# A two-layer hybrid transformer block: more block sums on VectorE, and chunk 3 of the last three feed-forward nets by seven block products

## The chip, the core and the metric

One core of a Trainium2 chip runs the whole program: two layers, batch 1, 256 tokens, all data in fp32. The core has five engines that run side by side, each with its own in-order stream of instructions: TensorE (PE, matrix products into PSUM; its weight loads appear as PEld), VectorE (DVE), ScalarE (ACT), GpSimd (POOL) and SyncE (SP, which here only issues transfers). Transfers run on 16 DMA engines. The metric is the device time of one execution in microseconds; the time of a kernel is the median of its runs.

## The reference

Each layer has a gated feed-forward net, a mixer (short convolution, a gated linear recurrence, multi-scale pooling), cross attention to 256 memory rows, and a second gated feed-forward net, each followed by a layer norm. The change touches the four feed-forward nets alone (two in each layer):

```python
D_MODEL = 1024; SEQ = 256; DEPTH = 2; D_FF = 2816

def swiglu(x, w_gate, w_up, w_down):
    return (jax.nn.silu(x @ w_gate) * (x @ w_up)) @ w_down

h = layer_norm(ALPHA * h + 0.5 * swiglu(h, ffn1_gate[l], ffn1_up[l], ffn1_down[l]), ln_g[l, 0], ln_b[l, 0])
...
h = layer_norm(ALPHA * h + 0.5 * swiglu(h, ffn2_gate[l], ffn2_up[l], ffn2_down[l]), ln_g[l, 3], ln_b[l, 3])
```

## The kernel before

**Products in three parts.** A weight block arrives in fp32 from memory. ScalarE rounds it to the matmul's fp32r type (the high part, tile `whi`, line 75) and VectorE subtracts that from the original (the low part, tile `wlo`, line 76). This pair is called a split here. A product is then the sum of three matmuls (high by high, high by low, low by high; `mm_rows`, line 132 through `product`). A split handles 128 x 1024 numbers, and there are eight `whi` and eight `wlo` buffers, so that ScalarE and VectorE can be at most eight splits ahead of TensorE.

**A feed-forward net.** The hidden width of 2816 is cut into five chunks of 512 (0 to 4) and one of 256 (chunk 5). For each chunk the kernel makes gate and up products with the 256 tokens (two tiles of 128), gates them, turns them (through a small transfer, `dealt`, and a transpose on VectorE into `square`), splits the result into `ah` and `al`, and later multiplies it by two slabs of the down matrix (`both`, four splits for the two slabs), which accumulate in four PSUM banks named `dn`. All other products go to the four PSUM banks named `acc`.

**Plain chunks.** `hidden` makes a chunk by 16 steps of gate and 16 of up: 96 matmuls of 512 columns and 8 splits.

**Chunks by seven block products.** `by_seven` uses a Strassen-like form. The two tiles of tokens, the two halves of the model width, gate and up give a 2 by 2 block product; seven products of blocks of tokens with blocks of weights take the place of eight. The sums of token blocks (`bx`, kept in `kTh` and `kTl`) are made once a net. The sums of weight blocks are made for each chunk, and every sum is split anew: 14 splits and 84 matmuls for 512 columns. With g0, g1 for the two halves of gate (`w00`, `w10`) and u0, u1 for those of up (`w01`, `w11`), the products take, in this order, g0; g0+u0; g1; g0+u0+u1; u0+u1; u1; g0+u0+u1+g1 (for chunk 5 the fifth and the sixth change places). VectorE makes g0+u0 and then adds u1, in place (`plus` in `parts_of`, line 736). u0+u1 is made by a transfer that GpSimd issues, which reads u1 from memory a second time and adds it onto u0 in SBUF (`more`, line 772). For the last sum another such transfer adds g1 in chunks of 512, and VectorE in chunk 5. Two slabs of the down product (`between`) lie between the products of each seven.

**Which chunks.** `sevens` says which: 2 and 4 in the first net, 2, 4 and 5 in the other three. `later` says after which plain chunk how many slabs of the down product follow.

**Where blocks are kept.** The four weight blocks of a seven have rotating homes: the pairs `spare0`/`spare1` and `lng`/`lnb`, and buffers of the pool `raw` (six); the first half of `w10` lies in `spare2`. A block loaded into a home must wait until the block before it there was last read.

**Order.** A scheduler places the instructions of each engine; inside an engine they run in that order. Transfers by SP run in the order of its queue too, and a queue entry whose home is not yet free holds up those behind it.

Of the kernel before, what the change touches and what calls it, by code (L numbers as in the profile page):

```python
# [60 lines left out]
def model(ctx: ExitStack, tc: tile.TileContext, t: dict, out: bass.AP):  # L61
# [6 lines left out]
    def acc(shape=(P, 2, SEQ), tag="acc"):  # L68
        return ps.tile(list(shape), F32, tag=tag, name=tag)
# [4 lines left out]
    def split(hi, lo, src):  # L74
        rounded = nc.scalar.copy(hi, src)  # L75
        lows.append(nc.vector.tensor_tensor(lo, src, hi.bitcast(F32), op=ALU.subtract))  # L76
        return rounded
# [78 lines left out]
    def mm_rows(o, xh, xl, wh, wl, start, stop, more=False):  # L156
        product(o, xh, wh, start, False, more)
        product(o, xh, wl, False, False, more)
        product(o, xl, wh, False, stop, more)
# [350 lines left out]
    def ffn(l, name, n, pend=None, last=False, early=None, started=None, following=None):  # L510
        gate, up, down = (t[f"{name}_{x}"][l] for x in ("gate", "up", "down"))
        with tc.tile_pool(name="ffn", bufs=2, reuse_waits="tile") as fp:
            acts = []
# [185 lines left out]
            def by_seven(c0, ncol, bx, between):  # L699
                deep = 1024 // ncol  # L700

                def rows_by_columns(r):
                    return r.rearrange("p (k c) -> p k c", c=ncol)

                def pieces(*tags):
                    return [
                        rows_by_columns(
                            (fp if "spare" in g else wp).tile([P, DM], F32, tag=g, name="raw", bufs=6 if g == "raw" else 1)
                        )
                        for g in tags  # L710
                    ]

                def part_of(m, j, i):
                    k = 4 * j + deep * i
                    return m[k * P : (k + deep) * P, c0 : c0 + ncol].rearrange("(k p) c -> p k c", p=P)

                def block(m, j, to):
                    for i, x in enumerate(to):
                        loads.append(nc.sync.dma_start(x, part_of(m, j, i)))
                    return to  # L720
# [8 lines left out]
                w01 = block(up, 0, pieces(*homes[1]))  # L729
                w10 = block(gate, 1, pieces(*homes[3]))  # L730

                def parts_of(r, plus=None):
                    hi, lo = [], []
                    for i in range(len(r)):
                        if plus is not None:
                            nc.vector.tensor_tensor(r[i], r[i], plus[i], op=ALU.add)
                        h = wp.tile([P, 1024], F32R, tag="whi", name="whi", bufs=8)
                        w = wp.tile([P, 1024], F32R, tag="wlo", name="wlo", bufs=8)
                        h, w = (rows_by_columns(x) for x in (h, w))
                        split(h, w, r[i])  # L740
                        hi.append(h)
                        lo.append(w)
                    return Weights(hi, lo, deep, [])

                def part_of_x(i, j):
                    d = slice(4 * j, 4 * j + 4)
                    return xTh[:, d, tok(i)], xTl[:, d, tok(i)]

                def run(o, x, w, more=False):
                    for k in range(4):  # L750
                        wh, wl = w.at(k, slice(0, ncol))
                        mm_rows(o, x[0][:, k, :], x[1][:, k, :], wh, wl, k == 0 and not more, k == 3, more)

                def put(o, a, op, b):
                    nc.vector.tensor_tensor(ordered(o), ordered(a), in_order(b), op=op)  # L755
# [8 lines left out]
                def bank():  # L764
                    return acc((P, CHUNK))[:, 0:ncol]

                def taken(o, bank):
                    return nc.scalar.copy(ordered(o), in_order(bank))

                def more(to, m, j):  # L770
                    for i, x in enumerate(to):
                        nc.gpsimd.dma_start(x, part_of(m, j, i), accum_op=ALU.add)  # L772

                o, total, one = (bank() for _ in range(3))
# [1 line left out]
                nc.scalar.copy(total, o)  # L776
                run(one, bx[0], parts_of(w00, w01))
                taken(e, one)
                more(w01, up, 1)
                run(o, part_of_x(0, 1), parts_of(w10), True)  # L780
                between[0]()
                activate(s, 0, o)
                w11 = block(up, 1, pieces(*homes[2]))
# [4 lines left out]
                copied = nc.scalar.mul(less, total, -1.0)  # L788
                between[1]()
                if ncol == CHUNK:  # L790
                    run(total, bx[2], parts_of(w01), True)
                    put(f, e, ALU.subtract, total)
                    run(less, bx[3], parts_of(w11), True)
                    run(total, part_of_x(1, 1), parts_of(w00), True)
                else:
                    run(less, bx[3], parts_of(w11), True)
                    run(total, bx[2], parts_of(w01), True)
                    put(f, e, ALU.subtract, total)
                    with tc.issue_after(copied.ins):
                        w = parts_of(w00, w10)  # L800
                    between[2]()
                    run(total, part_of_x(1, 1), w, True)
# [42 lines left out]
            def slab(c, u, fine=False):  # L845
                w = load(down, c * 4 + 2 * u, 2, 0, DM, fine, dealt=c < len(chunks) - 1)
                ah, al = acts[c]
                return w, ah[:, 2 * u : 2 * u + 2, :], al[:, 2 * u : 2 * u + 2, :]


            sevens = (2, 4) if early is not None else (2, 4, 5)
            passed, dealts, turn_memory = [], [], None
            bx = []

# [14 lines left out]
            def both(c, u, a=None, steps=range(2)):  # L869
                a = a or slab(c, u)  # L870
                for i in range(NT):
                    for k in steps:
                        for m in range(2):
                            apart = last and i == m == k == u == 1 and c == 3
                            rows_of(a, i, k, m, c == u == k == 0, apart)

            todo = [(c, u) for c in range(4) for u in range(2)]
            later = (0, 0, 0, 2, 0, 2) if early is None else (0, 1, 0, 1, 0, 2)
            for c, (c0, ncol) in enumerate(chunks):
                if not c:  # L880
                    acts.append(first()())
                    ys = [[acc((P, 512), "dn") for _ in range(2)] for _ in range(NT)]
                elif c in sevens:
                    half = []

                    def deal_last():
                        acts[4] = acts[4]()

                    left = by_seven(
                        c0, ncol, bx,  # L890
                        [lambda: both(*todo.pop(0))] * 2 if ncol == CHUNK else
                        [lambda: (half.append(slab(3, 0)), both(3, 0, half[0], (0,))), deal_last, lambda: both(3, 0, half[0], (1,))],
                    )
                else:
                    acts.append(hidden(c0)() if ncol == CHUNK else last_hidden(c0, turn_memory))
                if c == 1 and early is None:
                    bx.extend(blocks_of_x())
                if c == 5:
                    gb = ln_params(l, n)
                if c == 1 and early is not None:  # L900

                    with tc.issue_after(loads[-1].ins):
                        rest = early(fp)
                if c == 3 and early is not None:
                    with tc.issue_after(lows[-1].ins):
                        rest[0]()
                    nc.gpsimd.tensor_copy(early_memory[:, 0:2048:256], acts[2][0][:, 0, 0:8].bitcast(F32))
                    turn_memory = load_memory(fp, loads[-1])
                if c in sevens:
                    if ncol < CHUNK:  # L910
                        held = []
                        with tc.issue_after(lows[-1].ins):
                            acts[4] = acts[4](held)
                    acts.append(left() if c + 1 in sevens else left()() if c == 5 else left()()())
                    if ncol < CHUNK:
                        with tc.issue_after(passed[-1][0].ins), tc.issue_after(passed[-1][1].ins):
                            held[0]()
                        both(3, 1)
                else:
                    for _ in range(later[c]):  # L920
                        both(*todo.pop(0))
# [589 lines left out]
```

## Time and profile before

| what | value |
|---|---|
| median of 3 runs | 1061.81 us (1061.22 to 1062.94) |
| the profiled execution, its own time | 1062.18 us |
| its span, from the first to the last instruction | 1060.5 us |
| mean granted TensorE clock | 0.998 |
| second, third and fourth net, from the transposes of their input to those of the next stage's (chain of waits) | about 361 to 528, 528 to 695, 884 to 1053 us |

In the tables by stretch a cell is busy us and, in brackets, instructions; PEclk is the granted clock as a share of full speed, DMA the busy share of the 16 DMA engines, and the last number GB/s. In a timeline a row is start, duration, engine, line, operation, tile written and tile read; what stands in square brackets is idle time before it and what ended it. A group's row ends with its idle time and the releasers. Matmuls overlap, so that a TensorE instruction's own duration (0.38 us) is longer than its step (see the chain). A row in the list of waits is: waiting engine, tile and line, what released it, us in total, times, longest.

### The profile page before, as it was taken

The numbers are of one execution on the slowest core, as the hardware profiler recorded it, in microseconds if no ns is written. First come the engines' busy times: TensorE is split into PE (matmuls) and PEld (weight loads), VectorE is DVE, ScalarE is ACT, GpSimd is POOL, SyncE is SP. The second block draws the span as 40 slices with busy tenths as digits, with TensorE's granted clock in tenths as the row PEclk, the third lists the DMA queues.
The fourth block names the chain that finished last, engine by engine and source line by source line (L and its number), as shares of the span: only waits on it lengthen the run. The fifth ranks groups of instructions, "written<-read, shape, count | busy, mean of one in ns | idle before, by whom it ended". The sixth has DMA issues, their size and how long they took to land.

```text
span 1060.5 us, 16438 instructions
## 1 busy us (share of the span) xinstructions
PE 1050.7 (99%) x5998; PEld 933.9 (88%) x5998; DVE 920.6 (87%) x1228; ACT 667.3 (63%) x917; POOL 99.6 (9%) x137
## 2 busy tenths in 40 slices
PE   9999999999999999999999999999999999999997
PEld 7888888989899888888888888998898998888896
DVE  6998898989898789897898887999898888898787
ACT  6675765677557556655675656666775665675661
POOL 8002001000100001010001001010001000000001
PEclk9999999999999999999999999999999999999999
DMA  9999984855675589988789988876637775799972
GB/s 362 297 284 298 271 276 147 260 174 160 216 261 202 167 280 227 348 208 224 239 297 260 336 220 216 266 233 227 200 114 237 250 240 170 242 288 307 237 198 70
DMA packets 142690, 252.11 MB, mean 238 GB/s; under 512 B 11377, under 2 KB 52113, under 8 KB 142609
## 3 DMA queue, kind: packets, MB, share of 16 engines
q1 hardware_dynamic: 130656, 228.89, 65.0%
q0 software_dynamic: 11376, 20.99, 11.4%
q10 hardware_dynamic: 576, 1.18, 0.3%
q8 instruction: 47, 0.77, 0.3%
q14 instruction: 35, 0.28, 0.1%
HBM read 234.50 MB, written 1.05 MB: 222 GB/s over the span
## 4 chain that ended last, share of the span: by engine, by line
PE 97%; DMA 1%; DVE 1%; issue 1%; POOL 0%; ACT 0%; DVEq 0%; POOLq 0%
PE acc L132 64%; PE dn L132 30%; DMA raw<-in_ffn_gate_dram 1%; PE acc L203 1%; PE dn L1174 0%; DVE wlo L76 0%; PE dn L1248 0%; DMA h<-in_x_dram 0%; PE acc L615 0%; PE dn L1247 0%; PE dn L1236 0%; PE acc L1316 0%; PE dn L1199 0%; POOL raw L772 0%; DVE h L423 0%
## 5 line engine op out<-in xcount | busy, mean ns | idle before, releaser
L76 DVE TENSOR_TENSOR wlo<-raw,whi 128x1024 fp32r<-128x1024 f32 (+1 forms) x452 | 532.9, 1209 | 56.6 <-ACT whi L75 50.9
L75 ACT CAST whi<-raw 128x1024 fp32r<-128x1024 f32 (+1 forms) x452 | 456.6, 1042 | 182.3 <-PE dn L132 44.9
L132 PE MATMUL acc<-whi,xT 128*128 128x512 f32 (+1 forms) x1064 | 313.8, 372 | 0.4 <-DVE halves L755 0.4
L132 PEld LDWEIGHTS acc<-whi,xT 128*128 128x128 f32 x1064 | 199.1, 189 | 27.5 <-DVE halves L755 0.8
L132 PE MATMUL acc<-wlo,xT 128*128 128x512 f32 (+1 forms) x532 | 197.9, 372 | 0.0
L132 PE MATMUL dn<-whi,ah 128*128 128x512 f32 x346 | 131.5, 380 | 0.0
L132 PE MATMUL dn<-wlo,ah 128*128 128x512 f32 x346 | 131.1, 379 | 0.0
L132 PE MATMUL dn<-whi,al 128*128 128x512 f32 x346 | 131.1, 379 | 0.0
L132 PE MATMUL acc<-xT,whi 128*128 128x512 f32 x480 | 118.6, 381 | 0.0
L132 PEld LDWEIGHTS acc<-wlo,xT 128*128 128x128 f32 x532 | 100.6, 189 | 13.3
L132 PEld LDWEIGHTS acc<-xT,whi 128*128 128x128 f32 x480 | 86.5, 190 | 9.5
L132 PE MATMUL dn<-whi,xT 128*128 128x512 f32 x288 | 87.2, 380 | 0.0
L132 PEld LDWEIGHTS dn<-whi,al 128*128 128x128 f32 x346 | 65.4, 189 | 9.2
L132 PEld LDWEIGHTS dn<-whi,ah 128*128 128x128 f32 x346 | 65.4, 189 | 8.9
L132 PEld LDWEIGHTS dn<-wlo,ah 128*128 128x128 f32 x346 | 65.4, 189 | 8.8
L132 PEld LDWEIGHTS acc<-xT,wlo 128*128 128x128 f32 x480 | 63.8, 191 | 3.8
L132 PE MATMUL acc<-xT,wlo 128*128 128x256 f32 x480 | 64.5, 275 | 0.0
L132 PE MATMUL acc<-whi,kTh 128*128 128x512 f32 (+1 forms) x176 | 62.0, 352 | 0.0
L132 PE MATMUL acc<-wlo,kTh 128*128 128x512 f32 (+1 forms) x176 | 61.7, 351 | 0.0
L132 PE MATMUL acc<-whi,kTl 128*128 128x512 f32 (+1 forms) x176 | 61.7, 351 | 0.0
L132 PEld LDWEIGHTS dn<-whi,xT 128*128 128x128 f32 x288 | 54.4, 189 | 7.5
L132 PE MATMUL dn<-wlo,xT 128*128 128x512 f32 x144 | 54.6, 379 | 0.0
(261 smaller groups left out, 1288.5 us busy)
## 6 DMA issues: line engine op xcount, KB each, us to landing
raw<-in_ffn_up_dram SPq DMA_DIRECT2D x88, 512.0 KB, 5.6
raw<-in_ffn_down_dram SPq DMA_DIRECT2D x88, 512.0 KB, 5.8
raw<-in_ffn_gate_dram SPq DMA_DIRECT2D x84, 512.0 KB, 5.7
raw<-in_w_in_dram SPq DMA_DIRECT2D x48, 512.0 KB, 4.6
dealt<-sg SPq DMA_DIRECT2D x80, 128.0 KB, 4.9
raw<-in_ffn_up_dram POOLq DMA_DIRECT2D x19, 512.0 KB, 6.3
raw<-in_ffn_gate_dram POOLq DMA_DIRECT2D x16, 512.0 KB, 8.3
raw<-in_ca_k_dram SPq DMA_DIRECT2D x16, 512.0 KB, 5.4
```

The lines of the kernel that those rows point to most:

```text
L75: rounded = nc.scalar.copy(hi, src)
L76: lows.append(nc.vector.tensor_tensor(lo, src, hi.bitcast(F32), op=ALU.subtract))
L132: turns.append(nc.tensor.matmul(o, w, x, start=start, stop=stop, skip_group_check=more))
L203: turns.append(nc.tensor.transpose(pt[:, k - 4 * j, :], of_k, unit))
```

## The change

Three edits in `ffn`:

- In every seven, u0+u1 is made by VectorE (`parts_of(w01, w11)`), and the adding transfer `more(w01, up, 1)` goes. The adding transfer of g1 stays.
- In the last three nets (`early is None`) chunk 3 is made by seven block products too, so chunks 2, 3, 4 and 5 are sevens in a row, and only chunks 0 and 1 are plain.
- `later` and the condition on the turn of chunk 4 follow from that: the two slabs that came behind plain chunk 3 are now inside its seven. The first net keeps sevens 2 and 4.

```diff
                 taken(e, one)
-                more(w01, up, 1)
                 run(o, part_of_x(0, 1), parts_of(w10), True)
...
                 if ncol == CHUNK:
-                    run(total, bx[2], parts_of(w01), True)
+                    run(total, bx[2], parts_of(w01, w11), True)
                     put(f, e, ALU.subtract, total)
...
                     run(less, bx[3], parts_of(w11), True)
-                    run(total, bx[2], parts_of(w01), True)
+                    run(total, bx[2], parts_of(w01, w11), True)
...
-            sevens = (2, 4) if early is not None else (2, 4, 5)
+            sevens = (2, 4) if early is not None else (2, 3, 4, 5)
...
-            later = (0, 0, 0, 2, 0, 2) if early is None else (0, 1, 0, 1, 0, 2)
+            later = (0, 0, 0, 0, 0, 0) if early is None else (0, 1, 0, 1, 0, 2)
...
-                    acts.append(left() if c + 1 in sevens else left()() if c == 5 else left()()())
+                    acts.append(left() if c == 4 and 5 in sevens else left()() if c == 5 else left()()())
```

How it moves the instructions. VectorE in the last net before, from the last splits of chunk 2 into chunk 3 (`wlo` is a split, `halves` and `sg` the gating, `raw<-raw` a block sum, `al` the split of the chunk's result):

```order
L76 TENSOR_TENSOR wlo<-raw,whi 128x1024 x6
L755 TENSOR_TENSOR halves<-halves,acc 128x512
L76 TENSOR_TENSOR wlo<-raw,whi 128x1024 x2
L755 TENSOR_TENSOR halves<-halves,acc 128x512
L76 TENSOR_TENSOR wlo<-raw,whi 128x1024 x2
L809 TENSOR_TENSOR sg<-sg,halves 128x1024
L76 TENSOR_TENSOR wlo<-raw,whi 128x1024 x4
L565 STREAM_TRANSPOSE square<-dealt 128x4x4x32 x2
L76 TENSOR_TENSOR wlo<-raw,whi 128x1024
L76 TENSOR_TENSOR al<-square,ah 128x1024
```

The same place now:

```order
L76 TENSOR_TENSOR wlo<-raw,whi 128x1024 x9
L755 TENSOR_TENSOR halves<-halves,acc 128x512
L736 TENSOR_TENSOR raw<-raw 128x1024 x2
L755 TENSOR_TENSOR halves<-halves,acc 128x512
L76 TENSOR_TENSOR wlo<-raw,whi 128x1024 x3
L808 TENSOR_TENSOR sg<-sg,halves 128x1024
L76 TENSOR_TENSOR wlo<-raw,whi 128x1024 x3
L736 TENSOR_TENSOR raw<-raw 128x1024 x3
L76 TENSOR_TENSOR wlo<-raw,whi 128x1024 x2
L565 STREAM_TRANSPOSE square<-dealt 128x4x4x32 x2
L76 TENSOR_TENSOR wlo<-raw,whi 128x1024 x2
L76 TENSOR_TENSOR al<-square,ah 128x1024
```

Five block sums now stand between the gating of chunk 2 and the split of its result, where there was none, and the splits there are chunk 3's of its seven.

ScalarE in the last net, chunk 3 as it is now (`whi` is a rounding; 776, 544, 787 and 768 read a product in PSUM):

```order
L787 ACTIVATE acc<-acc 128x512
L75 CAST whi<-raw 128x1024 x10
L544 ACTIVATE sg<-acc 128x512
L75 CAST whi<-raw 128x1024 x2
L776 COPY acc<-acc 128x512
L75 CAST whi<-raw 128x1024 x3
L544 ACTIVATE sg<-acc 128x512
L75 CAST whi<-raw 128x1024
L75 CAST ah<-square 128x1024
L75 CAST whi<-raw 128x1024
L787 ACTIVATE acc<-acc 128x512
L768 COPY halves<-acc 128x512
```

Chunk 3 had two of these operations (544, twice) and has five now; each stands among roundings, and those behind it wait for it.

GpSimd's transfers in the last net, before and now:

```order
-L772 DMA raw<-in_ffn_up_dram 128x2x512 x2
-L772 DMA raw<-in_ffn_gate_dram 128x2x512 x2
-L772 DMA raw<-in_ffn_up_dram 128x2x512 x2
-L772 DMA raw<-in_ffn_gate_dram 128x2x512 x2
-L772 DMA raw<-in_ffn_up_dram 128x4x256
+L772 DMA raw<-in_ffn_gate_dram 128x2x512 x6
 L559 DMA dealt<-both 32x8x64 x2
```

Nine adding transfers a net become six, all of gate.

## The prediction

> **What bounds the kernel now.** I read the page's busy times and its chain of waits first, then the stretches of the three nets that get the fourth block product, and there the idle time of VectorE. The page (busy us, share, instructions; then the chain by engine):
>
> ```profile
> PE 1050.7 (99%) x5998; PEld 933.9 (88%) x5998; DVE 920.6 (87%) x1228; ACT 667.3 (63%) x917; POOL 99.6 (9%) x137
> ...
> PE 97%; DMA 1%; DVE 1%; issue 1%; POOL 0%; ACT 0%; DVEq 0%; POOLq 0%
> ```
>
> TensorE sets the time, but VectorE is close behind, so I ask how close it is where the change puts its work. The table by stretch has one row for each of the last three nets, from the second product of chunk 2 to the last split of a weight block:
>
> ```profile
> core 0: us, PE busy (x) PEld busy (x) DVE busy (x) ACT busy (x) POOL busy (x), PEclk, DMA share, GB/s
> 409.30:521.50 112.20, 111.79 (x558) 98.56 (x557) 96.32 (x94) 70.36 (x80) 9.88 (x9) 1.00 0.90 261
> 576.80:688.30 111.50, 111.50 (x558) 98.60 (x557) 95.39 (x93) 70.41 (x80) 9.87 (x9) 1.00 0.88 260
> 932.20:1042.50 110.30, 110.30 (x553) 97.56 (x552) 95.04 (x94) 68.33 (x78) 9.88 (x9) 1.00 0.84 246
> ```
>
> TensorE is full there. VectorE has 15.9, 16.1 and 15.3 us to spare in the three. At the end of a stretch there is no stock of split weights left. These are the last split of the last net on VectorE and the first matmul that reads it, from the timelines of the two engines:
>
> ```profile
> 1041.33 1.21 DVE L76 TENSOR_TENSOR wlo<-raw,whi 128x1024 fp32r<-128x1024 f32 x1
> ```
> ```profile
> 1043.26 0.38 PE L132 MATMUL dn<-wlo,ah 128*128 128x512 f32 x1
> ```
>
> The split ends at 1042.54 and TensorE wants it at 1043.26 (the fifth of the six matmuls of output tile 0 that read this slab; the six begin at 1042.40). The margin is 0.7 us. Whatever VectorE is late by at that point, beyond 0.7 us, the kernel is late by. So each stretch lasts as long as the longer of two sums: TensorE's matmuls, or VectorE's work with the waits that it cannot shed.
>
> **What the change takes from TensorE.** Chunk 3 by two plain products takes 2 x 2 x 8 x 3 = 96 matmuls of 512 columns, by seven block products 7 x 4 x 3 = 84: 12 fewer in each of three nets. The chain of waits gives the pace:
>
> ```profile
> 950.17 28.49 PE acc L132 x132
> ```
>
> 28.49 / 132 = 0.2158 us. The change takes off 12 x 0.2158 = 2.6 us a net, 7.8 us in all. That is the whole possible gain, if nothing else becomes late.
>
> **What it adds to VectorE.** VectorE's groups by line and shape (count | busy us, mean ns):
>
> ```profile
> L76 DVE TENSOR_TENSOR wlo<-raw,whi 128x1024 fp32r<-128x1024 f32 x444 | 527.3, 1218 | 56.1 <-ACT whi L75 50.6 <-PE acc L132 1.9 <-DMA lng<-in_ln_g_dram 0.6
> L736 DVE TENSOR_TENSOR raw<-raw 128x1024 f32<-128x1024 f32 x41 | 49.5, 1217 | 0.4
> ...
> L548 DVE TENSOR_TENSOR sg<-acc,sg 128x512 f32<-128x512 f32 x24 | 15.9, 680 | 0.0
> ...
> L755 DVE TENSOR_TENSOR halves<-halves,acc 128x512 f32<-128x512 f32 x16 | 10.9, 680 | 1.0 <-PE acc L132 1.0
> L809 DVE TENSOR_TENSOR sg<-sg,halves 128x1024 f32<-128x1024 f32 x8 | 9.7, 1218 | 0.0
> ```
>
> Neighbours overlap a little, so I take the step from one to the next. From the timeline:
>
> ```profile
> 949.68 4.63 DVE L76 TENSOR_TENSOR wlo<-raw,whi 128x1024 fp32r<-128x1024 f32 x4 [1.30 <-ACT whi L75]
> 954.23 0.68 DVE L755 TENSOR_TENSOR halves<-halves,acc 128x512 f32<-128x512 f32 x1
> 954.83 2.35 DVE L76 TENSOR_TENSOR wlo<-raw,whi 128x1024 fp32r<-128x1024 f32 x2
> ```
>
> (4.63 - 1.22) / 3 = 1.137 us for 1024 elements, 954.83 - 954.23 = 0.60 us for 512. In each of the last three nets VectorE gets, all inside the stretch:
> - sums of the second and fourth block in chunks 2, 3 and 4: 3 x 2 adds, and 1 in chunk 5, all of 1024 elements: 7 x 1.137 = 8.0 us;
> - chunk 3's own block sums (first with second, first with fourth): 4 adds, 4.5 us;
> - chunk 3's splits, 14 in place of 8: 6 x 1.137 = 6.8 us;
> - chunk 3's gating: two subtractions or additions from PSUM and one product of 1024 elements, for two products from PSUM: 2 x 0.60 + 1.14 - 2 x 0.60 = 1.1 us.
>
> Together 20.5 us a net (rounded up from 20.47), against 15 to 16 us that are free. This alone turns the order of the two engines round: in the second of these nets VectorE then has 95.4 + 20.5 = 115.9 us of work, TensorE 111.5 - 2.6 = 108.9. The wait that comes in is TensorE's, at the first matmul of a block that VectorE has not yet split. Its own queue is held behind it, the partial sums of the down projection too; what is late next is each chunk's copy and gating on ScalarE and VectorE, then the net's last product and the normalisation.
>
> **Which waits VectorE keeps.** In that same stretch before, VectorE's waits (us in total, times, longest), and the three rows that waited behind an addition:
>
> ```profile
> DVE wlo L76 <- ACT whi L75: 13.3, 13, 2.4
> DVE square L565 <- DMA dealt<-sg: 0.7, 1, 0.7
> DVE al L76 <- ACT ah L75: 0.7, 1, 0.7
> DVE both L809 <- ACT both L544: 0.4, 1, 0.4
> DVE halves L755 <- PE acc L132: 0.3, 1, 0.3
> ```
> ```profile
> 580.41 3.50 DVE L76 TENSOR_TENSOR wlo<-raw,whi 128x1024 fp32r<-128x1024 f32 x3 [1.17 <-ACT whi L75]
> ...
> 628.23 2.52 DVE L76 TENSOR_TENSOR wlo<-raw,whi 128x1024 fp32r<-128x1024 f32 x2 [0.51 <-ACT whi L75]
> ...
> 671.42 1.23 DVE L76 TENSOR_TENSOR wlo<-raw,whi 128x1024 fp32r<-128x1024 f32 x1 [1.49 <-ACT whi L75]
> ```
>
> Most of the 13.3 us is VectorE ahead of its time: ScalarE may not round the next block, because all eight buffers hold blocks that TensorE has not yet used. These waits vanish once TensorE waits for VectorE. What stays is the way of data: 2.1 us in the four small groups, and add, rounding on ScalarE, subtraction one after the other, 1.17 + 0.51 + 1.49 = 3.2 us. I take 5.3 us. Below, 2.1 us (other work put between hides every one of the 3.2), or at the very least 0; above, all 16 us (VectorE waits as long as ever, for other reasons).
>
> **The other parts.** ScalarE gets 6 more roundings a net and some PSUM copies, near 8 us by its row below; its 70 busy us of 111 in the stretch cover that, and if ScalarE were ever last, it would show as a longer VectorE wait, which the upper end holds. Of the adding transfers, 19 of the second block go and 6 of the first block come (2 for chunk 3 in each of three nets). Nothing on the path waits for the old ones but 0.41 us of TensorE's idle time in the first stretch (112.20 - 111.79); I count 0, and 0.4 us as the most to win. SP's loads of chunk 3 are the same eight tiles of 512 KB, moved to other homes; a block that comes late costs at most one landing, 5.6 us by the loads' row, once a net, and that too lies within the upper end.
>
> ```profile
> L75 ACT CAST whi<-raw 128x1024 fp32r<-128x1024 f32 x444 | 451.5, 1049 | 182.0 <-PE dn L132 44.9 <-PE acc L132 44.3 <-DVE raw L736 29.6
> ```
> ```profile
> raw<-in_ffn_up_dram SPq DMA_DIRECT2D x88, 512.0 KB, 5.6
> ...
> raw<-in_ffn_up_dram POOLq DMA_DIRECT2D x19, 512.0 KB, 6.3
> raw<-in_ffn_gate_dram POOLq DMA_DIRECT2D x16, 512.0 KB, 8.3
> ```
>
> The first net gets only 4 adds (chunks 2 and 4), 4.5 us. Its stretches:
>
> ```profile
> 55.00:82.00 27.00, 27.00 (x127) 23.65 (x126) 24.51 (x24) 20.05 (x23) 2.37 (x2) 1.00 1.04 305
> 82.00:149.00 67.00, 67.00 (x328) 59.07 (x328) 59.14 (x71) 44.31 (x50) 7.76 (x9) 1.00 0.97 274
> ```
>
> Idle are 2.5 and 7.9 us, and a plain chunk stands between the two sevens, in which VectorE catches up. I count 0; without that cover it would be 4.5 us.
>
> **The sum.** Each stretch becomes work before + 20.5 + 5.3: 122.1, 121.2 and 120.8 us, for 112.2, 111.5 and 110.3: +9.9, +9.7, +10.5, together +30.1 us. The profiled execution took 1062.18 us (1060.5 of span), 0.37 above the median of 1061.81. So 1092.3, or **1092 us** beside that median, 2.8% slower.
>
> **The clock.** The trace shows TensorE at half pace once, at its start: a 512-column matmul takes 0.78 us at 5.21 and 0.38 at 8.88.
>
> ```profile
> 5.21 0.78 PE L596 MATMUL dn<-kTh 128*128 128x512 f32 x1
> ...
> 8.88 0.38 PE L132 MATMUL dn<-wlo,xT 128*128 128x512 f32 x1
> ```
>
> [...]
>
> **Rivals.**
> 1. VectorE's spare time hides the additions, and the gain of TensorE comes through: 1062 - 7.8 = 1054 us. It needs the added work to stay under 108.9 - 95.4 - 5.3 = 8.2 us a net; no change in time needs it under 10.8. For it speaks the page's 87%, with 13% of the span free. Against it: the 11 adds alone are 12.5 us, and the 0.7 us margin at the stretch's end. 7 in 100, of which 3 for ending near no change, where an unseen stock of split blocks covers most.
> 2. VectorE loses every wait: 3 x 20.5 - (15.9 + 16.1 + 15.3) = +14 us, 1076 us. Against it: dealing through memory and the order add, round, subtract stay in the code. 6 in 100.
> 3. The two engines' waits couple: ScalarE takes its work in order, its copies of TensorE's results stand ahead of roundings, TensorE is now late, so the roundings are late and VectorE waits as long as before: + 3 x 20.5 = +61.5 us, 1124 us. For it: half of ScalarE's idle time in its row above is for TensorE (89 of 182 us). Against it: in ScalarE's changed order, shown with the change, most copies stand behind several roundings for the products that follow, so VectorE has splits in hand while ScalarE waits. 8 in 100, a part of it between the two figures.
> 4. TensorE's waits gather and halve its clock: by the two rows 3.7 us at half pace, 1.8 us lost, once in each of nine sevens: +16.5 us on top, 1108 us. 3 in 100.
>
> That the change does not happen is excluded by the order shown above: the fourth seven is there. The forecast keeps 76 in 100. A difference of 0.2% (2 us) is about what can be told from none. Faster is 0.04, within 0.2% 0.03, slower 0.93. Of the range, 1078 is near rival 2, with just under 1 us of waits left a net, and 1112 has 12 us of waits left a net, which takes in rival 4.
>
> **What would show it.** Right: TensorE with 30 us or more of idle time, waiting for VectorE's splits in chunks 3, 4 and 5 of the last three nets; VectorE over 93% busy from chunk 2 to the net's end; its waits for ScalarE's rounding down from 13 us to some 3 in each stretch; the first net's end within 2 us of where it was; 55 more instructions of 1024 elements on L736 and L76 together. Wrong: a TensorE that stays full to the ends of the nets (then a stock of split blocks was there that I did not see), or VectorE idle for more than 12 us in a stretch (rival 3), or a clock below 1.00 there (rival 4).

## The result, and the profile after

The changed kernel takes **1096.62 us** (median; 1095.32 to 1098.52) against 1061.51 for the kernel before: 1.0329 times as long, interval 1.0316 to 1.0341. The forecast was 1092 us in a range of 1078 to 1112. The profiled execution took 1096.27 us with a span of 1094.5.

Busy times on the page of the changed kernel, then its chain of waits by engine:

```profile
PE 1057.3 (97%) x5962; PEld 928.4 (85%) x5962; DVE 980.8 (90%) x1286; ACT 685.8 (63%) x944; POOL 84.6 (8%) x124
...
PE 51%; issue 29%; DMA 8%; DVE 7%; ACT 2%; POOL 1%; SPq 0%; DVEq 0%; POOLq 0%; ACTq 0%
```

TensorE has 36 matmuls fewer, and yet 6.6 us more busy time (1057.3 against 1050.7): three times its clock was halved, which adds some 5 us by the granted clock (last section), and a matmul that waits or is followed by a wait counts its own 0.38 us and not the step of 0.22. It now stands idle for 1094.5 - 1057.3 = 37.2 us, before for 9.8. Its share of the chain falls from 97% to 51%. VectorE has 60.2 us more.

The same three stretches as in the prediction, from the second product of chunk 2 to the last split of the net (us, busy us of TensorE, of the weight load, of VectorE, ScalarE and GpSimd with instructions, then clock, DMA share, GB/s):

```profile
410.50:535.30 124.80, 114.92 (x550) 98.14 (x549) 115.45 (x113) 77.05 (x89) 8.71 (x8) 0.99 0.79 232
589.50:710.20 120.70, 113.41 (x553) 96.65 (x552) 114.36 (x111) 76.15 (x89) 8.69 (x8) 1.00 0.79 237
953.50:1077.10 123.60, 114.87 (x544) 98.11 (x542) 114.12 (x111) 74.80 (x87) 8.72 (x8) 0.97 0.74 219
```

They are 12.6, 9.2 and 13.3 us longer than before, 35.1 in all: the whole loss sits in them (the span of the profiled execution is 34.0 us longer). VectorE is free for only 9.4, 6.3 and 9.5 us where it had 15 to 16, and TensorE, which was full, is idle for 9.9, 7.3 and 8.7. TensorE's waits in the whole run (waiting tile and line, what released it, us, times, longest):

```profile
PE acc L132 <- DVE wlo L76: 9.6, 10, 1.8
PE acc L132 <- DVE halves L755: 5.9, 5, 1.6
PE dn L132 <- ACT whi L75: 4.6, 4, 1.2
PE acc L132 <- ACT whi L75: 4.3, 6, 1.3
PE acc L132 <- ACT acc L776: 1.7, 2, 0.8
```

The kernel before had 0.4 us of waits for `halves` and none for splits. With 1.0 us more for splits of the down product (`dn`, `wlo`), 10.6 of these 27 us are for VectorE's splits, 5.9 for its subtraction into `halves`, and 10.6 for ScalarE's roundings and copies. And what VectorE itself waits for in the first of the three stretches:

```profile
DVE wlo L76 <- ACT whi L75: 7.5, 6, 2.6
DVE al L76 <- ACT ah L75: 1.1, 1, 1.1
DVE both L755 <- PE acc L132: 0.5, 1, 0.5
```

### The profile page after: what moved, and what is told of

It is laid out like the page before. It is cut to its first block, busy times and chain, and to the rows that moved or that the text cites. A ratio compares the mean times of both kernels' runs of the same rounds, so it can differ in the third digit from the quotient of the medians.

```text
span 1094.5 us, 16453 instructions
## 1 busy us (share of the span) xinstructions
PE 1057.3 (97%) x5962; PEld 928.4 (85%) x5962; DVE 980.8 (90%) x1286; ACT 685.8 (63%) x944; POOL 84.6 (8%) x124
## 4 chain that ended last, share of the span: by engine, by line
PE 51%; issue 29%; DMA 8%; DVE 7%; ACT 2%; POOL 1%; SPq 0%; DVEq 0%; POOLq 0%; ACTq 0%
PE acc L132 34%; PE dn L132 15%; DMA raw<-in_ffn_gate_dram 4%; DVE wlo L76 4%; ACT whi L75 1%; DVE raw L736 1%; POOL raw L772 1%; DMA raw<-in_ffn_down_dram 1%; DMA raw<-in_ffn_up_dram 1%; DMA dealt<-sg 1%; DMA dealt<-both 1%; PE acc L203 1%; PE dn L1173 0%; PE dn L1247 0%; DVE square L565 0%
## 5 line engine op out<-in xcount | busy, mean ns | idle before, releaser
L76 DVE TENSOR_TENSOR wlo<-raw,whi 128x1024 fp32r<-128x1024 f32 (+1 forms) x470 | 550.8, 1212 | 38.1 <-ACT whi L75 35.4
L75 ACT CAST whi<-raw 128x1024 fp32r<-128x1024 f32 (+1 forms) x470 | 469.9, 1040 | 172.2 <-DVE raw L736 79.2
L132 PE MATMUL acc<-whi,xT 128*128 128x512 f32 (+1 forms) x944 | 282.2, 375 | 8.2 <-DVE halves L755 5.9
L132 PEld LDWEIGHTS acc<-whi,xT 128*128 128x128 f32 x944 | 178.2, 191 | 35.0 <-issue 4.6
L132 PE MATMUL acc<-wlo,xT 128*128 128x512 f32 (+1 forms) x472 | 176.5, 374 | 1.6 <-DVE wlo L76 1.6
L132 PEld LDWEIGHTS acc<-wlo,xT 128*128 128x128 f32 x472 | 90.4, 192 | 13.7 <-DVE wlo L76 2.1
L736 DVE TENSOR_TENSOR raw<-raw 128x1024 f32<-128x1024 f32 x78 | 93.0, 1221 | 0.2
L132 PE MATMUL acc<-wlo,kTh 128*128 128x512 f32 (+1 forms) x224 | 81.7, 365 | 8.0 <-DVE wlo L76 8.0
L132 PE MATMUL acc<-whi,kTh 128*128 128x512 f32 (+1 forms) x224 | 81.4, 363 | 3.8 <-ACT whi L75 3.8
L132 PE MATMUL acc<-whi,kTl 128*128 128x512 f32 (+1 forms) x224 | 80.9, 361 | 0.0
L132 PEld LDWEIGHTS dn<-wlo,ah 128*128 128x128 f32 x346 | 65.7, 190 | 12.8 <-DVE wlo L76 3.9
```

The costliest lines, as they stand in the source:

```text
L132: turns.append(nc.tensor.matmul(o, w, x, start=start, stop=stop, skip_group_check=more))
```

## The experiments

**A common measure.** For all kernels I use one interval, a whole net: from the first addition of token tile 1 in the stage before (L381) to the net's own first addition. For the kernel before, then for the changed kernel, the tables by stretch:

```profile
360.66:521.74 161.08, 160.67 (x792) 141.52 (x791) 141.14 (x149) 103.57 (x121) 13.25 (x12) 1.00 0.86 254
528.01:688.41 160.40, 160.40 (x792) 141.63 (x791) 142.31 (x150) 102.43 (x120) 13.23 (x12) 1.00 0.87 262
883.50:1043.89 160.39, 160.39 (x792) 141.60 (x791) 140.53 (x149) 101.65 (x119) 13.25 (x12) 1.00 0.82 241
```
```profile
361.85:535.17 173.32, 163.44 (x783) 140.79 (x782) 160.18 (x167) 110.32 (x130) 9.64 (x9) 0.99 0.74 225
540.97:710.27 169.30, 162.01 (x785) 139.41 (x784) 161.02 (x168) 108.00 (x129) 9.61 (x9) 1.00 0.77 238
904.49:1077.87 173.38, 164.62 (x781) 141.62 (x780) 159.73 (x168) 108.53 (x128) 9.65 (x9) 0.98 0.70 214
```

Read so for every kernel, with means over the last three nets in us (VectorE free = net less VectorE busy; the runs are explained one by one below):

| kernel | sevens | median us | ratio | net | VectorE busy | VectorE free |
|---|---|---|---|---|---|---|
| before | 2, 4, 5 | 1061.5 | 1 | 160.6 | 141.3 | 19.3 |
| e1: sums only | 2, 4, 5 | 1063.9 | 1.0018 | 160.4 | 146.4 | 14.0 |
| e10: half dose on loads | 2, 4, 5 | 1064.8 | 1.0025 | 161.3 | 149.8 | 11.5 |
| e9: full dose on loads | 2, 4, 5 | 1075.6 | 1.0115 | 164.0 | 158.6 | 5.4 |
| e8: half dose | 2, 4, 5 | 1087.8 | 1.0248 | 169.4 | 150.3 | 19.2 |
| e7: full dose | 2, 4, 5 | 1095.8 | 1.0321 | 171.8 | 159.3 | 12.5 |
| e3: no second sum | 2 to 5 | 1071.8 | 1.0091 | 163.6 | 152.7 | 10.9 |
| e2: seven only | 2 to 5 | 1074.3 | 1.0125 | 165.8 | 152.7 | 13.0 |
| e11: e2, last sum by VectorE | 2 to 5 | 1080.8 | 1.0166 | 167.7 | 155.1 | 12.6 |
| after | 2 to 5 | 1096.6 | 1.0329 | 172.0 | 160.3 | 11.7 |
| e12: after, last sum by VectorE | 2 to 5 | 1099.9 | 1.0352 | 173.1 | 162.5 | 10.6 |
| e5: no transfer | 2 to 5 | 1110.1 | 1.0471 | 176.0 | 166.6 | 9.4 |
| e4: sum on GpSimd | 2 to 5 | 1113.9 | 1.0502 | 177.0 | 166.6 | 10.4 |
| e6: u1 by transfers | 2 to 5 | 1127.6 | 1.0624 | 179.7 | 147.7 | 32.1 |

Theory 1 is the prediction's: VectorE's work plus waits that it cannot shed set the stretch. The first four runs split the change into its two parts.

**e1: the transfer alone.** On the kernel before:

```diff
-                more(w01, up, 1)
...
-                    run(total, bx[2], parts_of(w01), True)
+                    run(total, bx[2], parts_of(w01, w11), True)
```

> The kernel before with the first edit alone: u0+u1 by VectorE in place of the adding transfer, sevens as before. Theory 1 (the time is VectorE's work plus the waits that it cannot shed, 6 to 9 us a stretch as measured after the change): each of the last three nets gets 5 adds, 5.7 us, and can shed 7 to 10 us of its 16 us of waits, so they stay as they are; the first net gets 4 adds and the 1.2 us by which it grew after the change: 1061 to 1064 us. Theory 2 (this edit carries the loss, since a sum on VectorE makes ScalarE's rounding wait for VectorE and so couples the engines): 1072 us or more, about a third of the loss of 35 us.

Measured 1063.86 us, ratio 1.0018 (1.0008 to 1.0028): Theory 1. Five additions a net cost some 2 us in all, and inside the last three nets nothing (160.4 us against 160.6). They lie in VectorE's free time.

**e2: the fourth seven alone.** On the changed kernel, the adding transfer put back:

```diff
+                more(w01, up, 1)
...
-                    run(total, bx[2], parts_of(w01, w11), True)
+                    run(total, bx[2], parts_of(w01), True)
```

> The changed kernel with u0+u1 by the adding transfer again: the second edit alone, chunk 3 by seven. Theory 1: VectorE gets 4 adds, 6 splits and 1.1 us of gating, 12.5 us a net, in place of 20.5; a stretch is 95.6 + 12.5 + 6 to 9 of waits = 114 to 117 us for 111.3: +3 to +6 a net, 1071 to 1080 us. Theory 3 (it is the row of sevens: homes that come free late, loads that land late, whatever VectorE's work is): within 6 us of the changed kernel, over 1090 us.

Measured 1074.32 us, 1.0125 (1.0109 to 1.0141), inside Theory 1's range; Theory 3 falls. So this part alone is 12.8 us slower although it has 36 matmuls fewer. The parts sum to some 2 + 12.8 = 15 us, the change costs 35.1: the two spend the same free time of VectorE, and only the first to come gets it for nothing.

**e3: neither transfer nor sum.** The changed kernel without the addition of u1 to u0 (that product is made with u0 alone):

```diff
-                    run(total, bx[2], parts_of(w01, w11), True)
+                    run(total, bx[2], parts_of(w01), True)
```

> The changed kernel without the sum u0+u1: the product takes u0 alone, neither VectorE nor a transfer adds u1, so part of the result is left out. TensorE's and ScalarE's work are those of the changed kernel, VectorE has 7 additions less in each of three nets and 4 less in the first. Theory 1: 24 us less VectorE work in the last three nets and most of the 1.2 us of the first: 1071 to 1077 us, and equal to the run with the adding transfer to 3 us. Theory 3: over 1090 us. If the adding transfer has a cost of its own, the run with the transfer is slower than this one by more than 3 us.

Measured 1071.82 us, 1.0091 (1.0076 to 1.0107). Against e2 the transfer itself is worth 2.5 us; the seven additions a net are worth 1096.6 - 1071.8 = 24.8 us, 8.3 a net (the four in the first net counted as nothing), where their own time by the prediction is 8.0. In these runs every microsecond of those additions shows.

e3 also shows what remains when the volume nearly fits. Its longest wait of TensorE in the second of the three nets, and VectorE and ScalarE ahead of it:

```profile
663.80 0.77 PE L132 MATMUL acc<-whi,xT 128*128 128x512 f32 x1 [3.43 <-DVE halves L755]
```
```profile
652.09 5.76 DVE L76 TENSOR_TENSOR wlo<-raw,whi 128x1024 fp32r<-128x1024 f32 x5
659.43 2.36 DVE L76 TENSOR_TENSOR wlo<-raw,whi 128x1024 fp32r<-128x1024 f32 x2 [1.58 <-ACT whi L75]
661.83 1.23 DVE L736 TENSOR_TENSOR raw<-raw 128x1024 f32<-128x1024 f32 x1
662.97 0.68 DVE L755 TENSOR_TENSOR halves<-halves,acc 128x512 f32<-128x512 f32 x1
```
```profile
658.36 1.99 ACT L75 CAST whi<-raw 128x1024 fp32r<-128x1024 f32 x2 [2.76 <-DMA raw<-in_ffn_gate_dram]
```

Follow it from the bottom: in chunk 4 the adding transfer of g1 lands late, ScalarE waits 2.76 us for it and VectorE 1.58. Behind these two splits in VectorE's order, after one more addition, stands the subtraction `f = e - total`, and TensorE's last product may not write into `total` before it. So TensorE waits 3.43 us for an instruction that does not need that block at all. Then its clock is halved (first matmul 0.77 us long, by stretch 0.50 and 0.70):

```profile
664.00:666.00 2.00, 2.00 (x5) 1.62 (x6) 1.78 (x3) 2.00 (x4) 0.00 (x0) 0.50 0.07 27
666.00:668.00 2.00, 2.00 (x8) 1.65 (x7) 2.00 (x3) 1.03 (x2) 0.00 (x0) 0.70 0.00 0
```

**e4: the sum on GpSimd.** `by=nc.gpsimd` for the additions of u1 to u0 in the changed kernel.

> The changed kernel with u0+u1 added by GpSimd in place of VectorE (7 additions in each of three nets, 4 in the first). No trace shows GpSimd at 128x1024. Theory 1: if GpSimd's additions are in time and take nothing from VectorE, as the run without the sum: 1071 to 1077 us. Rival: GpSimd takes several us for each, or slows VectorE while it runs, and the product waits for it: 1090 us or more.

Measured 1113.91 us, 1.0502 (1.0483 to 1.0522): the rival, and worse than VectorE doing it itself. GpSimd's additions and VectorE's two largest groups:

```profile
L736 POOL TENSOR_TENSOR raw<-raw 128x1024 f32<-128x1024 f32 x25 | 71.8, 2878 | 291.1 <-DMA raw<-in_ffn_up_dram 247.9 <-ACT whi L75 28.0 <-DVE raw L736 13.9
```
```profile
L76 DVE TENSOR_TENSOR wlo<-raw,whi 128x1024 fp32r<-128x1024 f32 x462 | 574.4, 1281 | 33.4 <-ACT whi L75 30.4 <-PE acc L132 1.9
L736 DVE TENSOR_TENSOR raw<-raw 128x1024 f32<-128x1024 f32 x53 | 81.0, 1540 | 0.2
```

An addition takes GpSimd 2.88 us, and VectorE's own additions stretch from 1221 ns (in e3) to 1540, the splits from 1221 to 1281. VectorE is busy 166.6 us a net where e3 has 152.7: 13.9 us more for seven additions that it does not make, and 8.0 if it made them. A single pair shows it, from the timelines of GpSimd and of VectorE:

```profile
655.29 2.36 POOL L736 TENSOR_TENSOR raw<-raw 128x1024 f32<-128x1024 f32 x1 [16.07 <-DMA raw<-in_ffn_up_dram]
```
```profile
655.42 3.31 DVE L736 TENSOR_TENSOR raw<-raw 128x1024 f32<-128x1024 f32 x1
```

VectorE's addition takes 3.31 us beside GpSimd's of 2.36; the addition before it, at 653.69 with none of GpSimd's beside it, takes 1.22. Why VectorE slows there the trace does not show.

**e5: no adding transfer at all.** On the changed kernel, g1 too is added by VectorE: `more(w00, gate, 1)` goes, and the last product takes `parts_of(w00, w10)`.

> The changed kernel with the third and last sum of each full chunk (g1 onto the first block) also made by VectorE, so that no adding transfer is left. Theory 1 (VectorE's own time is the bound in the last three nets): 6 more additions of 1.14 us in each of these nets, +20.5 us in all, less the waits behind the late transfer of g1, which are at most 9.3 us (25.2 us of waits measured in the three stretches, less 3 times the 5.3 us that I took as fixed): 1107 to 1118 us. Theory 2 (the late transfers are what holds the changed kernel, VectorE's work only lets them be late): 1097 us or less.

Measured 1110.14 us, 1.0471 (1.0434 to 1.0509): Theory 1. VectorE's work rises by 6.3 us a net, the net by 4.0; the rest came out of its free time (11.7 to 9.4 us).

**e6: more adding transfers.** The changed kernel with u1 added by transfers to both blocks that want it, in the full chunks:

```diff
+                if ncol == CHUNK:
+                    more(w00, up, 1)
+                    more(w01, up, 1)
...
-                run(total, bx[1], parts_of(w00, w11), True)
+                run(total, bx[1], parts_of(w00) if ncol == CHUNK else parts_of(w00, w11), True)
```

(In the full chunks the fifth product is again made with `parts_of(w01)`. This variant does not return the reference's result; its edit leaves no sum out, and the runs do not show which one goes wrong, so it tells about time alone.)

> The changed kernel, but in the full chunks u1 is added by transfers to both blocks that want it (g0+u0 and u0), so that VectorE makes one sum of each full chunk, g0+u0. VectorE's added work against the kernel before is then 2 sums of chunk 3, less 4 sums of chunks 2 and 4, plus 1 sum in the last chunk, 6 splits and 1.1 us of gating: 6 operations of 1.137 us, some 7 us a net, below the 10.6 us that are free beside the waits. Theory 1 (VectorE's time decides, and what fits in costs nothing): PE's 36 matmuls fewer show, 1054 to 1062 us. Rival (a transfer that lands 8.5 to 12 us after its issue is waited for by VectorE, which stands in order behind it): 2 to 6 us at each of the nine full sevens, 1068 to 1105 us.

Measured 1127.56 us, 1.0624 (1.0595 to 1.0653), worse than the rival's range. VectorE has only 147.7 us of work a net, and the net takes 179.7. ScalarE's first line of waits, and the adding transfers on GpSimd's queue (last number: us to landing):

```profile
ACT whi L75 <- DMA raw<-in_ffn_up_dram: 84.6, 27, 7.6
```
```profile
raw<-in_ffn_up_dram POOLq DMA_DIRECT2D x44, 512.0 KB, 9.3
raw<-in_ffn_gate_dram POOLq DMA_DIRECT2D x22, 512.0 KB, 9.9
```

An adding transfer that the next product but one needs is not free: it lands after 9.3 us, and everything behind it on ScalarE and VectorE waits. In the kernel before, 19 and 16 such transfers landed after 6.3 and 8.3 us, in the changed kernel 22 of g1 after 8.5; that the number on the queue makes the difference is not shown.

**e7 and e8: a dose of VectorE's work in the kernel before.** Sevens and sums untouched; `tensor_tensor(r, r, r, max)` ahead of splits, 18 and 9 times a net.

> The kernel before, its sevens, sums and transfers untouched, with 18 extra VectorE operations of 128x1024 in each of the last three nets (the larger of a block and itself, ahead of the splits): 20.5 us of VectorE's work a net, as the change adds, and no matmul fewer. Theory 1 (VectorE's time alone): stretch of 96.3+20.5+5.3 = 122.1 us against 112.2, so about +10 us a net: 1088 to 1102 us. Rival (the four sevens in a row and their transfers are what costs, VectorE's time is a part only): 1062 to 1080 us.

> The kernel before with 9 such extra VectorE operations in each of the last three nets, 10.2 us a net. Theory 1 (free time of 15.1 to 15.9 us less 5.3 us of waits, so that 10.2 us just fit): 1061 to 1067 us. Rival (VectorE is coupled to PE and ScalarE so tightly that each added microsecond shows from the start): half of the full dose's loss or more, 1075 us or more.

Measured 1095.80 us (1.0321, 1.0306 to 1.0337) and 1087.82 us (1.0248, 1.0233 to 1.0263). The full dose came out as Theory 1 had it, the half dose as the rival had it, 26.5 us for 27 operations of 1.14 us. Half a dose cannot cost three quarters of a whole one if only the amount counts, so I looked at VectorE's waits in e8 (L736 is the added operation):

```profile
DVE raw L736 <- DMA raw<-in_ffn_up_dram: 31.4, 4, 10.3
DVE wlo L76 <- ACT whi L75: 29.9, 30, 3.3
```

I had put the operation on u0+u1 as well, the block that an adding transfer fills. VectorE now waited for that transfer itself, up to 10.3 us, 31.4 us in all, more than the whole loss. e7 has 22.1 + 6.6 us of the same waits (u1 and g1). Both doses were spoilt, and e7's agreement with Theory 1 was chance.

**e9 and e10: the dose on plain loads.** The same numbers of operations on g1 and u1, which plain loads bring well ahead:

```diff
-                run(o, part_of_x(0, 1), parts_of(w10), True)
+                run(o, part_of_x(0, 1), parts_of(w10, extra=2 if ncol == CHUNK else 1), True)
...
-                    run(less, bx[3], parts_of(w11), True)
+                    run(less, bx[3], parts_of(w11, extra=2 if ncol == CHUNK else 1), True)
```

(For e10 one operation a piece in the full chunks, and in the last chunk on u1 alone.)

> The kernel before with the same 18 extra VectorE operations in each of the last three nets, but all on the two blocks that come by plain loads well ahead (g1 and u1; two on each piece of the full chunks, one on each of the last), none on a block that an adding transfer fills. Theory 1 (VectorE's own time): stretch of 96.3+20.5+5.3 = 122.1 us against 112.2: 1088 to 1102 us. Rival (the extra work itself is mostly hidden, the loss of the earlier doses was VectorE standing behind the transfers): 1080 us or less.

> The same with 9 extra operations a net (one on each piece of g1 and u1 in the full chunks, one on u1 in the last), 10.2 us a net. Theory 1, with the 31 us that VectorE stood behind transfers in the earlier half dose taken as its whole loss: 10.2 us fit into what is free beside the waits, 1061 to 1068 us. Rival (each added microsecond shows from the start, at half of the full dose's loss or more): 1075 us or more.

Measured 1075.56 us (1.0115, 1.0092 to 1.0138) and 1064.77 us (1.0025, 1.0013 to 1.0037). The half dose is hidden but for 2.5 us, as Theory 1 says. The full dose costs 13.3 us, not 30: the rival's side. Its nets, which are uneven:

```profile
363.81:526.03 162.22, 161.25 (x791) 141.27 (x790) 157.37 (x166) 102.06 (x119) 13.24 (x12) 1.00 0.86 252
532.04:699.21 167.17, 162.83 (x792) 142.57 (x791) 161.48 (x169) 101.73 (x120) 13.23 (x12) 0.99 0.86 251
895.46:1058.01 162.55, 160.89 (x789) 141.06 (x788) 156.96 (x165) 100.17 (x118) 13.25 (x12) 1.00 0.81 238
```

VectorE works nearly as long as in the changed kernel (158.6 against 160.3 us), but it is left with 5.4 us of free time, not 11.7. So two things make the change's loss: the amount of VectorE's work, and 6.3 us a net more than in e9 in which, with four sevens, VectorE stands idle though it is late. The two kernels also differ in ScalarE's copies and in g1's transfers; that the row of sevens itself does it is argued and not shown.

**e11 and e12: is it the late transfer of chunk 4?** On e2 and on the changed kernel, in chunk 4 of the last three nets only:

```diff
+                own = early is None and c0 == 4 * CHUNK
-                if ncol == CHUNK:
+                if ncol == CHUNK and not own:
                     more(w00, gate, 1)
...
-                    run(total, part_of_x(1, 1), parts_of(w00), True)
+                    run(total, part_of_x(1, 1), parts_of(w00, w10) if own else parts_of(w00), True)
```

> The kernel with chunk 3 by seven and the second plus fourth block by the adding transfer (1074.32 us when it was run), but in chunk 4 of the last three nets the first block plus g1 is made by VectorE: 2 additions of 1.14 us more a net, and the adding transfer that lands last is gone. Theory 1 (VectorE's amount of work decides): 3 times 2.3 us more, 1074 to 1082 us. Theory 4 (the loss sits in one place: VectorE's splits of that late block stand ahead of the subtraction for which TensorE waits 4.3 to 5.0 us, and the clock is halved after it, 1.7 us): 6 to 6.7 us a net come back, 1054 to 1060 us, faster than the kernel before.

> The changed kernel with that same edit: in chunk 4 of the last three nets g1 is summed by VectorE, 2 additions more a net, the late transfer gone. Theory 1 (VectorE's amount of work decides): 1099 to 1104 us. Theory 4 (the late transfer, the waits it brings TensorE and the clock halved behind them carry a third or more of the 35 us): 1080 to 1092 us.

Measured 1080.83 us (1.0166, 1.0147 to 1.0186) and 1099.90 us (1.0352, 1.0335 to 1.0368): Theory 1 both times, and Theory 4 falls. The late transfer was gone, and the waits behind it, but VectorE's free time fell only from 11.7 to 10.6 us a net, for 2.2 us of additions. In the second of the three nets of e12:

```profile
610.25 1.22 DVE L76 TENSOR_TENSOR wlo<-raw,whi 128x1024 fp32r<-128x1024 f32 x1 [2.58 <-ACT whi L75]
...
679.93 1.23 DVE L76 TENSOR_TENSOR wlo<-raw,whi 128x1024 fp32r<-128x1024 f32 x1 [1.87 <-ACT whi L75]
...
691.76 2.36 DVE L76 TENSOR_TENSOR wlo<-raw,whi 128x1024 fp32r<-128x1024 f32 x2 [1.39 <-ACT whi L75]
697.50 1.23 DVE L76 TENSOR_TENSOR wlo<-raw,whi 128x1024 fp32r<-128x1024 f32 x1 [1.11 <-ACT whi L75]
```

The changed kernel has there 2.48, 2.57 (the late transfer) and 1.11. Much of what the transfer gave back came again as waits of VectorE for ScalarE's rounding, which itself waits for VectorE's additions (L75 in the changed kernel: 79.2 of 172.2 us of ScalarE's idle time, before 29.6 of 182.0):

```profile
L75 ACT CAST whi<-raw 128x1024 fp32r<-128x1024 f32 (+1 forms) x470 | 469.9, 1040 | 172.2 <-DVE raw L736 79.2 <-DMA raw<-in_ffn_gate_dram 21.5 <-PE acc L132 14.2
```

No version came out faster than the kernel before. Among the six kernels with four sevens in the table, from e3 to e5, VectorE's work rises by 13.8 us a net and the net by 12.3: 0.9 us for each. In e5, which has no adding transfer, 9.4 us are still free. In these six the free time stays between 9.4 and 13 us (in e6, which waits for transfers, it is 32.1); which link of addition, rounding, split and PSUM copy fixes its size I did not settle.

## Why the prediction was right, and where it was not

1. *VectorE comes to bound the last three nets, with a loss of some 10 us each.* Right: 12.6, 9.2 and 13.3 us, for 9.9, 9.7 and 10.5. TensorE's wait was forecast for blocks not yet split, but those are 10.6 of its 27 us; ScalarE, for which it waits as long, itself waits for VectorE's additions (79.2 us, before 29.6). The 35.1 us of the result against 30.1 forecast are the sum of the next two points.
2. *20.5 us of added work a net.* Nearly right: 115.45, 114.36 and 114.12 us in the stretches, where work before + 20.5 gives 116.8, 115.9 and 115.5. It is 1.4 us less because before, many operations stood alone (1.22 us), and now they follow each other (1.137 us): VectorE's idle gaps in the three stretches fall from 23, 24 and 23 to 9, 7 and 9.
3. *Kept waits of 5.3 us.* This is the term that was mis-sized: 9.4, 6.3 and 9.5 us, a mean of 8.4. I had taken the add, round, subtract waits as they stood before, three of them with 3.2 us, and that size held: 4.5, 1.1 and 4.5 us in the three stretches, a mean of 3.4. What the sum lacks is the wait behind g1's adding transfer, which I had counted as 0: 3.0, 5.1 and 3.2 us. ScalarE and then VectorE, in chunk 4 of the first of these nets:

```profile
498.18 1.99 ACT L75 CAST whi<-raw 128x1024 fp32r<-128x1024 f32 x2 [3.91 <-DMA raw<-in_ffn_gate_dram]
```
```profile
499.26 2.36 DVE L76 TENSOR_TENSOR wlo<-raw,whi 128x1024 fp32r<-128x1024 f32 x2 [2.56 <-ACT whi L75]
```

So 3 x (8.4 - 5.3) = 9.3 us more from waits and 4.3 less from work make the difference of 5.0; that the two errors partly cancel is luck.
4. *No stock of split blocks, so each microsecond beyond the free time is lost.* It holds for the change (e3 to after: 8.3 us a net for 8.0 of additions), but not as a general reading of that profile: e9 puts the same 20.5 us into the kernel before and loses 13.3 us, 4.4 a net (3.4 by the nets' own lengths). By steps 2 to 4 it should have lost 10. Two simplifications lay in the working that e9 does not have to pay for: the stretch was closed at its start, though VectorE has 4 us free ahead of it in the net (161.08 - 112.20 = 48.9 us long, 141.14 - 96.32 = 44.8 busy), and the kept waits were taken as fixed, where e9 comes down to 5.4 us in the whole net. For the change itself they happened not to matter, since it keeps more waits than I took: that part of the agreement is luck.
5. *The change's other parts at nothing.* The transfers of u0+u1 cost little indeed (2.5 us, e2 against e3). That nothing waits for those of g1 was wrong: in the changed kernel VectorE waits some 11 us behind them in the three stretches (point 3), though making these sums on VectorE instead costs more (e5, e12). The first net, taken at 0, ends 1.2 us later (its first transpose of tile 1 at 173.20, before at 172.01), within the 2 us that I gave; in e9, whose first net is the kernel before's, the same group of transposes starts 1.3 us later too (173.12 for 171.84), so this cannot be told from none.
6. *Rivals.* Rival 1 (the spare time hides the work) holds for e1 and e10, not for the change: their 5.1 and 8.5 us of added VectorE time fit. Rival 2 is refuted by the waits left. Rival 3 (waits stay whole) is true in its mechanism, not in its size: of 15 to 16 us about 8.4 stayed, and e9, with 5.4 us left in a whole net, speaks for their belonging to the coupled engines and not to VectorE alone. Rival 4 (halved clock) happened, in three places in place of nine, some 5 us in place of 16.5: last section. That TensorE's clock falls after waits was an assumption: the two rows of the trace before show half pace at the start of the run alone. e3 (a wait of 3.43 us, then a clock of 0.50) and the changed kernel show it, though not after every wait (last section).
7. *The signs to look for.* The 55 more instructions came (L736 from 41 to 78, the 1024-element splits from 444 to 462). TensorE is idle for 25.9 us in the three stretches, short of the 30 named, since another part of the loss is busy time: half clock, and matmuls around a wait. VectorE is busy for 92.5, 94.7 and 92.3% of the stretches, over 93% in one only; its waits for rounding fell from 12.3, 13.3 and 13.0 to 7.5, 6.2 and 7.7 us, not to 3. These two were the signs of point 3.

## What to carry to other kernels

An engine's free share is not a stock to spend: ask first in which order its instructions stand, and what chain of two engines (addition here, rounding there, subtraction here) each added instruction lengthens; the same 20.5 us cost 13 us as work on blocks that were there early and 35 us within the change, four sevens and all. Two edits that each fit into the free time of an engine need not fit together, so their prices must be summed against that time once (here some 2 and 12.8 us alone, 35.1 together). When a test dose is put on an engine, put it on data that has long landed, or the dose measures the transfer (in e8 31.4 us of VectorE's waits, where the loss was 26.5).

## What the hardware showed that I had not expected

**The clock falls without one long wait.** In e3 a single wait of 3.43 us came ahead of half clock (0.50). In the changed kernel none of TensorE's waits above was longer than 1.8 us, and yet its clock was halved once in the first and twice in the third of the three nets. In the first:

```profile
503.40:506.80 3.40, 0.75 (x2) 0.37 (x2) 3.40 (x4) 3.36 (x5) 0.00 (x0) 1.00 0.06 22
506.80:508.50 1.70, 1.56 (x12) 1.56 (x13) 1.70 (x3) 0.82 (x1) 0.00 (x0) 0.90 0.56 168
508.50:510.20 1.70, 1.70 (x10) 1.70 (x9) 1.70 (x2) 0.37 (x1) 0.00 (x0) 0.50 0.86 155
510.20:512.00 1.80, 1.80 (x8) 1.57 (x7) 1.22 (x2) 0.87 (x2) 0.00 (x0) 0.62 0.87 307
```

In 3.4 us TensorE was busy for 0.75 us, in two matmul records; some 1.3 us later the clock went to half, for about 3.4 us, which costs 1.7 us. Three waits, of 1.31, 0.84 and 0.80 us with one matmul record between each and the next, stood here where e3 had the one of 3.43.

How much work keeps the clock up, these runs do not show. Nearly the same share of work in 3.4 us came before half clock in the third net (first two rows) and was followed by full clock in the first (last two):

```profile
1012.40:1015.80 3.40, 1.14 (x6) 0.42 (x4) 3.40 (x4) 2.64 (x4) 0.00 (x0) 1.00 0.31 99
1016.70:1018.40 1.70, 1.70 (x6) 1.05 (x5) 1.70 (x3) 1.70 (x2) 0.00 (x0) 0.51 0.45 78
...
469.10:472.50 3.40, 1.15 (x4) 0.48 (x3) 3.40 (x4) 2.66 (x4) 0.00 (x0) 1.00 0.35 110
472.50:475.90 3.40, 2.91 (x14) 2.22 (x13) 3.40 (x4) 3.40 (x4) 0.00 (x0) 1.00 0.39 77
```
